# Score and output products of attention issued one by one between the products of the next weight block

## The chip, the cores and the metric

The kernel runs on one core of one Trainium2 chip. The metric is the device time of one execution, in microseconds (us). A core has TensorE (PE in the profile, with its load of stationary operands shown apart as PEld), VectorE (DVE), ScalarE (ACT), GpSimd (POOL) and SyncE (SP), which in this kernel only issues DMAs. Each engine works through its own instructions in the order in which they were written; semaphores make one engine wait for another.

## The reference

A decoder trunk of two layers on 256 positions of width 2048, all in float32. Layer 0 mixes by trailing-window pooling, layer 1 by causal block attention (MoBA) with one block of 256 keys, so that it is plain causal attention over 12 heads of width 128 here. Both layers also have a memory branch: 4 heads that attend to 256 memory tokens. In short:

```python
def memory_attention(mq, mem, w_mem_kv):
    mk, mv = jnp.split(mem @ w_mem_kv, 2, axis=-1)
    ...
    s = jnp.einsum('bshd,bmhd->bhsm', q, k).astype(jnp.float32) * (HEAD_DIM ** -0.5)
    p = jax.nn.softmax(s, axis=-1).astype(v.dtype)
    return jnp.einsum('bhsm,bmhd->bshd', p, v).reshape(B, S, MEM_WIDTH)
```

Each layer has one input projection into [main branch | its SiLU gate | memory query | its SiLU gate], the two gated branches are put side by side, one output projection follows, then `x = LN(alpha * x + y)`. MoBA's keys and values come from one shared projection of the stream behind layer 0; its scores are masked causally and go through the same softmax and value product.

## The kernel before

Every product is done in three: an operand is split into a high part (ScalarE copies it into the rounded type, line 102) and a low part (VectorE subtracts, line 103), and high x high, high x low and low x high are accumulated. So `mm` at line 98 carries every product.

The work is a list of items, one for each weight block of 1024 columns by 128 rows. `run` walks through the list; step i does this: split the block of item i + 3 (`prep_piece`), issue the loads that are planned for this step, then let item i consume its block, then call the functions that were put down for this step with `later(n, fn)`, n steps ahead. For a projection, consuming is 12 products of 512 columns (two row tiles, two k tiles, three products each, lines 240 to 242) into two accumulators; after the eighth block `done` takes the accumulators over. Split weight blocks have four buffers, so VectorE and ScalarE run at most three blocks ahead of TensorE. A few items carry no products: they only bring in blocks of the last output projection ("keep").

Queries, keys and gates have to be turned: VectorE transposes 32 x 32 blocks, SP writes the tile to DRAM with four DMAs (`via<-tr`, line 260), reads it back one step later (`dd<-via`, line 263), and five steps after `done` it is split (`put`). Values are split straight from the accumulators (`to_values`, tile `vv`) by ScalarE and VectorE when the last value block is done.

Attention works on pairs of heads, `MemPair` for the memory branch and `MobaPair` for layer 1. `plan(pr, a, c)` puts their stages on the steps, counted from the last query block: `a` the 12 score products (tile `s`) with the mask and the maxima on VectorE, `a + 1` the exponentials on ScalarE, `a + 2` the division, `a + 3` the turn of the probabilities through DRAM (`p<-via`), `a + 8` their split into halves (`ph`, `pl`), `c` the 12 output products (tile `o`) and the gating, which writes the input of the output projection (`zf`, `zh`, `zl`). There are two memory layers with two pairs each and three MoBA groups with two pairs each: 10 pairs, so 20 blocks of 12 products. In a memory pair all products have 256 columns; in a MoBA pair half have 256 and half 128, since half of a causal score row is known to be masked. A block of 12 is issued in one piece between the products of step a (or c) and those of the next step. The first pair starts at step 6 and the second at 15; the outputs come at 16 and 25 in memory layers and at 17 and 25 in MoBA groups.

After the last query block come eight blocks of the gate and, in a MoBA group, eight of the values, so the last value block is item 16 of that count; in the second and third group a keep item lies among them, and it is item 17.

PSUM holds four accumulators, one bank for `o`, two for `s` (tile name `s2`) and one for `pt`.

## Time and profile before

| | |
|---|---|
| median of 3 runs | 813.2 us |
| lowest and highest | 812.97 and 815.07 us |
| time of the profiled execution | 814.67 us |
| its span, first to last instruction | 812.9 us |
| TensorE busy in the span | 791.9 us, 3671 products |
| VectorE, ScalarE busy | 546.6 us, 390.3 us |
| granted TensorE clock, mean | 0.995 |

The span of the profiled execution is 1.8 us shorter than its time, and its time is 1.5 us above the median. In a timeline row stand start, length, engine, line, operation, tile written and tiles read, shape and count; a bracket gives the idle time of the engine in front of it and what ended it. The length of a product is its way through the array and longer than the distance from one product to the next, so costs are read from starts.

### The profile page before, as it was taken

How to read it: one execution, taken by the hardware profiler on the slowest of the kernel's cores; microseconds unless marked ns; L12 is line 12 of the kernel's file. 1: busy time of each engine (PE TensorE's matmuls, PEld its weight loads, DVE VectorE, ACT ScalarE, POOL GpSimd, SP SyncE). 2: the span in 40 equal slices, each digit the busy share in tenths (PEclk: the TensorE clock that was granted, in tenths of full speed). 3: DMA queues.
4: the chain of work that ended last, by engine and by line, in shares of the span. 5: the costliest groups of instructions: out<-in, count | busy, mean ns of one | idle time of the engine just before them, and what ended most of it. 6: DMA issues, size and time to landing. Idle time of an engine off the chain costs nothing.

```text
span 812.9 us, 10023 instructions
## 1 busy us (share of the span) xinstructions
PE 791.9 (97%) x3671; PEld 660.1 (81%) x3671; DVE 546.6 (67%) x710; ACT 390.3 (48%) x502; POOL 0.2 (0%) x4
## 2 busy tenths in 40 slices
PE   7999999999999999998999999999999999999996
PEld 6878888888888888886778888888887888878885
DVE  6666676768775665755768867666576656765936
ACT  6545545544454434584545544545454445544510
POOL 0000000000000000000000000000000000000000
PEclk9999999999999999999999999999999999999998
DMA  8999666766687755689998786868574685756632
GB/s 321 365 338 310 204 211 194 253 201 215 211 272 262 250 199 187 211 295 293 385 318 258 257 298 207 284 208 271 182 229 139 199 272 197 245 159 219 207 104 103
DMA packets 96180, 193.69 MB, mean 238 GB/s; under 512 B 8671, under 2 KB 31487, under 8 KB 95871
## 3 DMA queue, kind: packets, MB, share of 16 engines
q1 hardware_dynamic: 94800, 190.61, 70.5%
q10 hardware_dynamic: 1332, 2.46, 0.9%
q8 instruction: 28, 0.46, 0.2%
q14 instruction: 20, 0.16, 0.1%
HBM read 173.37 MB, written 19.66 MB: 237 GB/s over the span
## 4 chain that ended last, share of the span: by engine, by line
PE 85%; DMA 8%; DVE 3%; ACT 2%; SPq 1%; issue 1%; DVEq 0%; ACTq 0%
PE acc L98 80%; DMA via<-tr 3%; PE o L98 2%; PE s L98 2%; DMA dd<-via 2%; DMA p<-via 1%; DMA zh<-in_w_in 1%; DVE wl L103 1%; DMA zl<-in_w_mv 1%; ACT wh L102 1%; SPq L260 1%; ACT p L327 1%; PE pt L98 1%; DVE tr L251 0%; DMA raw<-in_w_mk 0%
## 5 line engine op out<-in xcount | busy, mean ns | idle before, releaser
L98 PE MATMUL acc<-wh,xh 128*128 128x512 f32 x704 | 275.3, 391 | 2.3 <-ACT wh L102 2.3
L98 PE MATMUL acc<-wl,xh 128*128 128x512 f32 x704 | 274.9, 391 | 1.5 <-DVE wl L103 1.5
L98 PE MATMUL acc<-wh,xl 128*128 128x512 f32 x704 | 274.5, 390 | 0.0
L103 DVE TENSOR_TENSOR wl<-raw,wh 128x1024 fp32r<-128x1024 f32 (+4 forms) x155 | 180.7, 1176 | 101.5 <-ACT wh L102 99.7
L102 ACT ACTIVATE wh<-raw 128x1024 fp32r<-128x1024 f32 (+4 forms) x155 | 157.2, 1022 | 160.5 <-PE acc L98 133.7
L98 PEld LDWEIGHTS acc<-wh,xh 128*128 128x128 f32 x704 | 132.6, 188 | 30.3 <-ACT wh L102 3.2
L98 PEld LDWEIGHTS acc<-wl,xh 128*128 128x128 f32 x704 | 132.6, 188 | 29.1 <-DVE wl L103 2.5
L98 PEld LDWEIGHTS acc<-wh,xl 128*128 128x128 f32 x704 | 132.4, 188 | 27.7
L98 PE MATMUL acc<-wl,zh 128*128 128x512 f32 x224 | 87.3, 390 | 0.0
L98 PE MATMUL acc<-wh,zh 128*128 128x512 f32 x224 | 87.3, 390 | 0.0
L98 PE MATMUL acc<-wh,zl 128*128 128x512 f32 x224 | 87.2, 389 | 0.0
L103 DVE TENSOR_TENSOR wl<-zh,wh 128x1024 fp32r<-128x1024 f32 x38 | 46.3, 1222 | 26.4 <-ACT wh L102 26.4
L103 DVE TENSOR_TENSOR wl<-zl,wh 128x1024 fp32r<-128x1024 f32 x39 | 47.4, 1221 | 20.1 <-ACT wh L102 20.0
L98 PE MATMUL acc<-wh,mh 128*128 128x512 f32 (+1 forms) x130 | 51.3, 395 | 5.1 <-ACT wh L102 5.1
L102 ACT ACTIVATE wh<-zl 128x1024 fp32r<-128x1024 f32 x39 | 40.7, 1057 | 28.1 <-PE acc L98 27.6
L102 ACT ACTIVATE wh<-zh 128x1024 fp32r<-128x1024 f32 x38 | 39.8, 1054 | 29.6 <-PE acc L98 28.1
L98 PE MATMUL acc<-wl,mh 128*128 128x512 f32 (+1 forms) x130 | 51.4, 395 | 0.8 <-DVE wl L103 0.8
L98 PE MATMUL acc<-wh,ml 128*128 128x512 f32 (+1 forms) x130 | 50.9, 392 | 0.0
L98 PEld LDWEIGHTS acc<-wl,zh 128*128 128x128 f32 x224 | 42.1, 188 | 8.8 <-DVE wl L103 0.3
L98 PEld LDWEIGHTS acc<-wh,zl 128*128 128x128 f32 x224 | 42.0, 188 | 8.8
L98 PEld LDWEIGHTS acc<-wh,zh 128*128 128x128 f32 x224 | 42.1, 188 | 8.6
L102 ACT ACTIVATE zh<-zf 128x256 fp32r<-128x256 f32 x32 | 12.9, 414 | 49.0 <-DVE zf L338 44.7
(152 smaller groups left out, 731.8 us busy)
## 6 DMA issues: line engine op xcount, KB each, us to landing
raw<-in_w_in SPq DMA_DIRECT2D x59, 512.0 KB, 6.1
raw<-in_w_out SPq DMA_DIRECT2D x58, 512.0 KB, 4.4
via<-tr SPq DMA_DIRECT2D x116, 128.0 KB, 3.1
zh<-in_w_in SPq DMA_DIRECT2D x26, 512.0 KB, 6.9
zl<-in_w_in SPq DMA_DIRECT2D x25, 512.0 KB, 6.6
dd<-via SPq DMA_DIRECT2D x21, 512.0 KB, 4.8
raw<-in_w_mk SPq DMA_DIRECT2D x10, 512.0 KB, 4.9
mh<-in_w_sk SPq DMA_DIRECT2D x10, 512.0 KB, 9.1
```

The source lines that it names most:

```text
L98: nc.tensor.matmul(o, l, r, start=start, stop=stop)
L102: nc.scalar.activation(hi, src, AF.Copy)
L103: nc.vector.tensor_sub(lo, src, f(hi))
L260: nc.sync.dma_start(st["via"][:, :, i].rearrange("j r x -> r j x"), tr[32 * i:32 * i + 32, :, :n])
L327: nc.scalar.activation(dst, src, AF.Exp, bias=self.nb[:, c:c + 1], scale=SCALE, accum_out=self.sm[:, c:c + 1])
```

## The change

Score and output products are no longer issued by their stage. The stage puts them into a queue, `woven`, and the next projection item takes one out behind each of its own 12 products of 512 columns. What used to follow the products within the stage becomes a stage of its own one step later, which first empties the queue: `scored` (mask, maxima) behind the scores and `gate` (gating, split) behind the outputs. Exponentials, division, turn and halves move one step with it. The outputs' step c changes for some pairs: from 17 to 18 for the first pair of each MoBA group, from 25 to 26 for the second pair everywhere, while the first pair of the memory layers stays at 16. Arithmetic, number and shapes of the products and the DMAs stay the same.

```diff
+    woven = deque()
+
+    def weave_mm(*args):
+        woven.append(args)
+
+    def tick():
+        if woven:
+            mm(*woven.popleft())
+
+    def flush():
+        while woven:
+            tick()
...
-                            mm(acc[t][:, s], xh, h[:, kk, s], first, False)
-                            mm(acc[t][:, s], xh, l[:, kk, s], False, False)
-                            mm(acc[t][:, s], xl, h[:, kk, s], False, last)
+                            for st, wt, a0, a1 in ((xh, h, first, False), (xh, l, False, False), (xl, h, False, last)):
+                                mm(acc[t][:, s], st, wt[:, kk, s], a0, a1)
+                                tick()
...
+        def gate(self):
+            flush()
+            for j in range(2):
+                gated(self.o[:, j], self.st["g"][:, self.h0 + j, :], self.kt0 + j)
...
         def a(self):
             q, k = self.st["q"], self.st["k"]
-            s = ps.tile([P, 2, 2, T], F32, name="s2")
+            s = self.s = ps.tile([P, 2, 2, T], F32, name="s2")
...
-                    mm(s[:, j, t], qh, k[:, 0, h], True, False)
-                    mm(s[:, j, t], qh, k[:, 1, h], False, False)
-                    mm(s[:, j, t], ql, k[:, 0, h], False, True)
+                    weave_mm(s[:, j, t], qh, k[:, 0, h], True, False)
+                    weave_mm(s[:, j, t], qh, k[:, 1, h], False, False)
+                    weave_mm(s[:, j, t], ql, k[:, 0, h], False, True)
+
+        def scored(self):
+            flush()
+            s = self.s
...
-                    mm(o[:, j], vh, self.ph[:, e], m == 0, False)
-                    mm(o[:, j], vh, self.pl[:, e], False, False)
-                    mm(o[:, j], vl, self.ph[:, e], False, m == 1)
-            for j in range(2):
-                gated(o[:, j], g[:, self.h0 + j, :], 12 + self.h0 + j)
+                    weave_mm(o[:, j], vh, self.ph[:, e], m == 0, False)
+                    weave_mm(o[:, j], vh, self.pl[:, e], False, False)
+                    weave_mm(o[:, j], vl, self.ph[:, e], False, m == 1)
...
     def plan(pr, a, c):
 
-        later(a, pr.a)
-        later(a + 1, pr.exps)
-        later(a + 2, pr.divide)
-        later(a + 3, pr.b)
-        later(a + 8, pr.halves)
+        for n, fn in enumerate((pr.a, pr.scored, pr.exps, pr.divide, pr.b)):
+            later(a + n, fn)
+        later(a + 9, pr.halves)
         later(c, pr.c)
+        later(c + 1, pr.gate)
...
             plan(prs[0], 6, 16)
-            plan(prs[1], 15, 25)
+            plan(prs[1], 15, 26)
...
-            plan(prs[0], 6, 17)
-            plan(prs[1], 15, 25)
+            plan(prs[0], 6, 18)
+            plan(prs[1], 15, 26)
```

`MobaPair` is changed in the same way as `MemPair`.

## The prediction

> **What bounds the kernel now.** I read the page first, then the waits of TensorE, then the timeline of TensorE around each of the places that the change touches. The page and the waits give:

> ```profile
> PE 791.9 (97%) x3671; PEld 660.1 (81%) x3671; DVE 546.6 (67%) x710; ACT 390.3 (48%) x502; POOL 0.2 (0%) x4
> ...
> PE acc L98 <- ACT wh L102: 7.4, 3, 5.1
> PE o L98 <- DVE vv L103: 1.8, 2, 0.9
> PE s L98 <- DVE qq L103: 0.8, 1, 0.8
> PE o L98 <- ACT vv L102: 0.6, 2, 0.4
> ```

> TensorE is busy for 97% of the span, so only two things can move the time: what a product costs in the stream, and the few microseconds in which TensorE stands still. Of the waits, three belong to score products `s` and output products `o`, 1.8 + 0.8 + 0.6 = 3.2 us. The waiting list counts only idle time; the cost of a stop is read from the distances between starts, which also hold the slow restart. A row of the timeline is the start, the length, the operation, and in brackets the idle time before it. The worst stop is that of the outputs in the second MoBA group:

> ```profile
> 614.48 0.39 PE L98 MATMUL acc<-wh,xl 128*128 128x512 f32 x1
> 615.10 0.39 PE L98 MATMUL o<-ph,vv 128*128 128x256 f32 x1 [0.23 <-ACT vv L102]
> 615.33 0.28 PE L98 MATMUL o<-pl,vv 128*128 128x256 f32 x1
> 616.49 0.44 PE L98 MATMUL o<-ph,vv 128*128 128x256 f32 x2 [0.88 <-DVE vv L103]
> 616.77 0.27 PE L98 MATMUL o<-pl,vv 128*128 128x128 f32 x1
> 617.09 0.49 PE L98 MATMUL o<-ph,vv 128*128 128x128 f32 x2
> ...
> 617.00:622.00 5.00, 4.96 (x19) 4.15 (x19) 2.57 (x10) 1.78 (x3) 0.00 (x0) 0.66 0.00 0
> ...
> 700.00:715.00 15.00, 13.70 (x71) 11.23 (x70) 10.56 (x16) 7.26 (x16) 0.00 (x0) 1.00 0.52 192
> ```

> The outputs follow the last product of the values directly, so they wait until ScalarE and VectorE have split those values. The last two rows are sums over stretches of time, and the number after the engines' busy times is the granted clock. From 617 to 622, right behind the stop, it is 0.66 on average; around the like stop at 711 it is 1.00.

> **The unit costs.** In the fences of this part stand an output block of a memory pair, a score block and the rest of an output block of MoBA pairs, none of them with a wait:

> ```profile
> 145.34 0.39 PE L98 MATMUL acc<-wh,xh 128*128 128x512 f32 x1
> ...
> 146.02 0.28 PE L98 MATMUL o<-ph,vv 128*128 128x256 f32 x1
> 146.13 0.28 PE L98 MATMUL o<-pl,vv 128*128 128x256 f32 x1
> ...
> 147.45 0.40 PE L98 MATMUL acc<-wh,xh 128*128 128x512 f32 x1
> 147.68 0.40 PE L98 MATMUL acc<-wl,xh 128*128 128x512 f32 x1
> ...
> 148.84 0.39 PE L98 MATMUL acc<-wh,xh 128*128 128x512 f32 x1
> ```

> ```profile
> 584.72 1.54 PE L98 MATMUL s<-kk,qq 128*128 128x128 f32 x12
> 586.10 0.40 PE L98 MATMUL acc<-wh,xh 128*128 128x512 f32 x1
> ...
> 641.64 0.34 PE L98 MATMUL o<-ph,vv 128*128 128x256 f32 x2
> 641.82 0.28 PE L98 MATMUL o<-pl,vv 128*128 128x128 f32 x1
> ...
> 642.74 0.44 PE L98 MATMUL acc<-wh,xh 128*128 128x512 f32 x1
> 643.02 0.40 PE L98 MATMUL acc<-wl,xh 128*128 128x512 f32 x1
> ```

> A 512-column product takes (146.02 - 145.34)/3 = 0.227 us. A 256-column one takes (147.45 - 146.02)/12 = 0.119. In the MoBA block six have 256 columns and six 128: (586.10 - 584.72)/12 = 0.115 on average, so a 128-column product takes 0.11 there, hardly less than twice the columns do. Something other than columns, about 0.11 us a product, holds it: the load of the next stationary block.

> **The change, part by part.**

> 1. *Alternation.* Twenty blocks of 12 products (8 of memory pairs, 12 of MoBA pairs) give 96 + 72 = 168 products of 256 columns and 72 of 128. No trace of before has long and short products in turn, so I bound it by the edges of blocks. Going in, the first 256-column product lasts 146.13 - 146.02 = 0.11; coming out, the first 512-column product lasts 147.68 - 147.45 = 0.23. A pair is 0.34, against 0.227 + 0.119 = 0.346 now. For 128 columns: behind a longer product it lasts (641.82 - 641.64) - 0.12 = 0.06, but the 512-column product behind a 128-column one lasts 643.02 - 642.74 = 0.28, since the load that the short product did not cover is paid there. Pair 0.34, now 0.227 + 0.11 to 0.115. So alternation is worth nothing in the likely case: the long product hides the short one's load, and the next long one's load stands behind the short product. Lower bound: every 256-column product at 0.113, 168 x 0.006 = 1.0 us won. Upper bound: the six products from 147.45 to 148.84 take 1.39 against 1.36, 0.03 us a block; half of that for every alternating pair is 240 x 0.015 = 3.6 lost, but since the two ends of a pair read 0.34, I cut this at 1.9 and take +0.1.

>  [...]

> 2. *Outputs of the second and third MoBA group.* They are queued one step later and then issued behind products of the step after it. Today's loss at 614: from the values' last product to the first output 615.10 - 614.48 - 0.227 = 0.39; 615.10 to 615.33 is 0.10 too long; 615.33 to 616.49 is 1.04 too long; 616.49 to 616.77 covers two products, 0.10 too long; 616.77 to 617.09 is 0.20 too long. Sum 1.83. The third group is the same:

> ```profile
> 710.64 0.39 PE L98 MATMUL acc<-wh,xl 128*128 128x512 f32 x1
> 711.40 0.39 PE L98 MATMUL o<-ph,vv 128*128 128x256 f32 x1 [0.37 <-ACT vv L102]
> 711.63 0.28 PE L98 MATMUL o<-pl,vv 128*128 128x256 f32 x1
> 712.79 0.45 PE L98 MATMUL o<-ph,vv 128*128 128x256 f32 x2 [0.88 <-DVE vv L103]
> 713.08 0.27 PE L98 MATMUL o<-pl,vv 128*128 128x128 f32 x1
> 713.39 0.49 PE L98 MATMUL o<-ph,vv 128*128 128x128 f32 x2
> ...
> 609.45 0.96 DVE L409 TENSOR_TENSOR p<-s,mask 128x768 f32<-128x768 f32 x1 [0.64 <-PE s L98]
> 610.44 1.01 DVE L322 TENSOR_REDUCE small<-p 128x2 f32<-128x256 f32 x2
> ...
> 615.75 1.28 DVE L103 TENSOR_TENSOR vv<-acc,vv 128x512 fp32r<-128x512 f32 x2
> ```

>  0.53 + 0.10 + 1.04 + 0.11 + 0.20 = 1.98. What covers it: after the values' last product at 614.48 comes a whole weight block (12 x 0.227 = 2.72 us) and one product more, so the first output starts at about 617.66; the split of the values ends at 617.03. The mask and maxima of the second pair, now one step later, stand on VectorE ahead of it: 12 products of scores and 12 of weights end about 612, plus 0.96 + 1.01 + 0.17 gives 614.4, a weight split (1.23, as long as the split of the same size at 419.85 below) to 615.6, values to 616.9. The low part is asked for by the third output only, at 618.35. Covered, by 1.4 us. If that cover were gone, the 1.83 and 1.98 would come back.

> 3. *The half clock.* 5 x (1 - 0.66) = 1.70 us of the profiled execution went into it. It began within a microsecond of the stop; that the stop at 711 had none behind it shows that a stop does not always bring it. Without a stop I expect none there; 0 and 1.70 are the bounds, and I take the 1.70.

>  [...]

> 4. *Scores of the second memory layer.*

> ```profile
> 419.36 0.39 PE L98 MATMUL acc<-wh,xl 128*128 128x512 f32 x1
> 419.87 0.50 PE L98 MATMUL s<-kk,qq 128*128 128x256 f32 x2
> 421.13 1.45 PE L98 MATMUL s<-kk,qq 128*128 128x256 f32 x10 [0.76 <-DVE qq L103]
> ...
> 419.85 1.23 DVE L103 TENSOR_TENSOR qq<-dd,qq 128x1024 fp32r<-128x1024 f32 x1 [3.18 <-ACT qq L102]
> ```

>  Loss now: 419.87 - 419.36 - 0.227 = 0.28, and 421.13 - 419.87 - 2 x 0.12 = 1.02, together 1.30. The queries come from a DMA, so their low half still ends at 419.85 + 1.23 = 421.08. The third score product is the first to read it; alternating, it would start at 419.59 + 3 x 0.227 + 2 x 0.12 = 420.5. It waits about 0.57, and with 0.10 for the slow restart, as in part 2, 0.67 stays: 0.63 won. Bounds: 0 to 1.30.

> 5. *Everything a step later.* Score reduction, exponentials, division, turn and halves all move one step, with their DMAs on SP's queue, and keep their distances from one another; no weight load passes another. VectorE stands in the same place relative to TensorE as now, waiting for scores (0.64 idle at 609.45), so its cover of later weight blocks is unchanged. One distance shrinks. In memory layers the first pair's outputs stay at step 16 while its halves move from 14 to 15, and the second pair's `scored` empties the queue in step 16, so these two blocks are not alternated at all. In the second memory layer the halves end, with the wait for their DMA, about 3.4 us ahead of the outputs:

> ```profile
> 446.51 1.23 DVE L103 TENSOR_TENSOR pl<-p,ph 128x1024 fp32r<-128x1024 f32 x1 [1.02 <-ACT ph L102]
> ...
> 451.11 0.28 PE L98 MATMUL o<-ph,vv 128*128 128x256 f32 x1
> ```

>  451.11 - 447.74 = 3.4, less one step of 2.72 leaves 0.7. Cost 0 if that holds, up to 1 us if the DMA is late; I take 0.25. The gate of the last group, a step or two later, lies at least three weight blocks ahead of the products that read it: nothing.

> Sum against the profiled execution's own 814.67 (its span is 812.9, and the 1.8 around it stay): -1.83 - 1.98 - 1.70 - 0.63 + 0.1 + 0.25 = -5.8, so 808.9. The median of the three runs is 813.2, 1.5 below the profiled one, nearly the half-clock loss; if those runs had none, 813.2 - 4.44 + 0.35 = 809.1. Both readings meet at 809.0.

> **The rivals.**

> - *The half clock appears elsewhere, or stays* (808.9 + 1.7 = 810.6). For it: the stops of TensorE for weights (7.4 us in the list) are untouched and could be hit. Against: they were not hit in this execution. 15%.
> - *Loads run two ahead.* Then a 128-column product costs 0.06 and nothing is paid behind it: 72 x 0.055 = 4.0, so 805.0. For it: the 0.06 above. Against: the 0.28 that follows. 7%. [...]
> - *The waits move.* VectorE gets to the values only after the mask and maxima; if it is over 1.4 us later than worked out, half of 1.83 + 1.98 comes back with part of the scores' wait, and with late halves in the second memory layer: 811.3 to 813. 14%.
> - *Slower: each change of length exposes a load.* If the 0.28 behind a 128-column product (0.057 above 0.227) is paid behind every short product, with no gain going in, it costs 240 x 0.057 = 13.7: 822.6. It turns the forecast into a loss from 4.2/240 = 0.018 us a pair. For it: that row, and the 0.03 after each block. Against: behind 256 columns the row shows 0.23. 14%.

> **How the numbers follow.** Forecast 809.0 with 50%. I call no change what lies within 0.3% (2.4 us, about what a measurement of this kernel can tell), 810.8 to 815.6. Faster: 50 + 7 + two thirds of 15 = 67%; no change: 5 + 14 and 1 of the slower rival = 20%; slower 13%. The range: downwards all of the 256-column gain (1.0), the whole score wait (0.67), none of the 0.35, and the lowest of the three runs as the base (0.2), 806.8; upwards the half clock and most of the moved waits, 812.2. Left out are two-ahead loads and the slower rival, 21%.

> **What would show it.** Waits of `o` on `vv` gone and that of `s` on `qq` down to about 0.6 us; no granted clock under 1.00 at 617; in an alternating block 12 pairs in 4.1 us (256 columns) and 4.1 (MoBA): much less speaks for loads two ahead, over 4.4 for the slower rival. A new wait of `o` on `pl` near 450, or of weights on ScalarE behind a block, would prove me wrong in part 5.

## The result, and the profile after

| | before | after |
|---|---|---|
| median, 13 runs each, in turn | 815.07 us | 811.25 us |
| lowest to highest | 812.97 to 819.53 | 809.68 to 813.82 |
| ratio of the times, 95% interval | | 0.9949 (0.9931 to 0.9967) |
| profiled execution, its span | 814.67, 812.9 | 812.46, 810.7 |
| granted TensorE clock, mean | 0.995 | 0.992 |

The change makes the kernel faster by 0.5%. The forecast was 809.0 against 813.2, a ratio of 0.9948. The median of before rose to 815.07 when more runs of it were made, so the absolute time lies 2 us above the forecast and the difference, 3.8 us, beside the 4.2 forecast.

The list of waits of TensorE in the kernel after, whole (engine, tile, line, what ended the wait, us in total, times, the longest):

```profile
PE acc L98 <- ACT wh L102: 6.2, 2, 5.0
PE acc L98 <- DVE wl L103: 3.9, 5, 2.4
PE pt L908 <- DVE cc L905: 2.7, 1, 2.7
PE acc L98 <- ACT cct L910: 0.4, 1, 0.4
```

No score product and no output product waits any more. Two of the four rows are waits for weights, and the other two (`pt` and `cct`, at 804 us) belong to the last normalization at the end of the kernel; three rows of `s` and `o` with 3.2 us are gone. To read what that was worth I take, in each kernel, the same two 512-column products on either side of a place and the time from one to the other. Between the two stands the same work in both kernels, so the difference is what the place costs. The timeline of TensorE before, two products around the scores of the second memory layer, then around the outputs of the second and the third MoBA group:

```profile
418.23 0.39 PE L98 MATMUL acc<-wh,xh 128*128 128x512 f32 x1
...
426.53 0.39 PE L98 MATMUL acc<-wh,xh 128*128 128x512 f32 x1
...
613.35 0.39 PE L98 MATMUL acc<-wh,xh 128*128 128x512 f32 x1
...
626.45 0.39 PE L98 MATMUL acc<-wh,xh 128*128 128x512 f32 x1
...
709.51 0.39 PE L98 MATMUL acc<-wh,xh 128*128 128x512 f32 x1
...
721.11 0.39 PE L98 MATMUL acc<-wh,zh 128*128 128x512 f32 x1
```

The same products in the timeline after:

```profile
421.26 0.39 PE L98 MATMUL acc<-wh,xh 128*128 128x512 f32 x1
...
428.18 0.39 PE L98 MATMUL acc<-wh,xh 128*128 128x512 f32 x1
...
615.54 0.39 PE L98 MATMUL acc<-wh,xh 128*128 128x512 f32 x1
...
625.17 0.39 PE L98 MATMUL acc<-wh,xh 128*128 128x512 f32 x1
...
708.45 0.39 PE L98 MATMUL acc<-wh,xh 128*128 128x512 f32 x1
...
718.08 0.39 PE L98 MATMUL acc<-wh,zh 128*128 128x512 f32 x1
```

The scores' stretch went from 8.30 to 6.92 us, the outputs of the second group from 13.10 to 9.63, those of the third from 11.60 to 9.63 (9.636 without rounding): 1.38 + 3.47 + 1.97 = 6.8 us won. But blocks that never waited became longer. Where TensorE alternates, the timeline after shows, first in a memory pair and then in a MoBA pair:

```profile
116.18 0.28 PE L98 MATMUL s<-kk,qq 128*128 128x256 f32 x1
116.29 0.40 PE L98 MATMUL acc<-wl,xh 128*128 128x512 f32 x1
...
120.06 0.28 PE L98 MATMUL s<-kk,qq 128*128 128x256 f32 x1
...
587.02 0.22 PE L98 MATMUL s<-kk,qq 128*128 128x128 f32 x1
587.08 0.45 PE L98 MATMUL acc<-wl,xh 128*128 128x512 f32 x1
587.36 0.22 PE L98 MATMUL s<-kk,qq 128*128 128x128 f32 x1
...
587.70 0.22 PE L98 MATMUL s<-kk,qq 128*128 128x128 f32 x1
```

Eleven pairs of 256 and 512 columns take 120.06 - 116.18 = 3.88 us, 0.353 a pair, where the two kinds in blocks of their own take 0.119 + 0.227 = 0.346. A pair of 128 and 512 takes 0.34: the short product lasts 587.08 - 587.02 = 0.06 and the long one behind it 587.36 - 587.08 = 0.28. By the same kind of stretch, a memory block or a block of MoBA scores that alternates costs 0.060 us more (memory scores 6.900 to 6.960, memory outputs 9.620 to 9.680, MoBA scores 6.833 to 6.893) and a block of MoBA outputs 0.083 (9.553 to 9.636). Of the 20 blocks 18 alternate, since the first pair's outputs in the memory layers are flushed in one piece: 12 x 0.060 + 6 x 0.083 = 1.2 us. Of that, 0.99 lies outside the three stretches above, so the places that the change touches come to -6.8 + 1.0 = -5.8 us.

The two profiled executions differ by only 814.67 - 812.46 = 2.2 us. Most of the missing 3.6 is in the stretch between the two layers (from the first product of the second layer's memory values to the first of its eighth query block), which the change leaves alone: 46.91 us before (355.00 to 401.91), 49.77 after (355.17 to 404.94). One wait is longer there in this execution, and after it two stretches of 3.41 us run at half clock (374.20 to 377.62 and 391.27 to 394.69). The timeline after, and sums over stretches of time (start, end, length; busy time and instructions of TensorE, its loads, VectorE, ScalarE, GpSimd; mean granted clock; DMA share; GB/s):

```profile
372.89 0.50 PE L98 MATMUL acc<-wl,mh 128*128 128x512 f32 x1 [2.38 <-DVE wl L103]
```

```profile
374.00:378.00 4.00, 4.00 (x12) 3.17 (x11) 1.22 (x1) 2.94 (x5) 0.00 (x0) 0.57 1.00 306
391.00:395.00 4.00, 3.81 (x10) 3.02 (x11) 4.00 (x5) 2.67 (x3) 0.00 (x0) 0.57 1.05 408
...
614.00:622.00 8.00, 8.00 (x40) 6.70 (x40) 6.01 (x11) 5.91 (x13) 0.00 (x0) 1.00 0.44 166
```

The clock behind the second group's outputs is now 1.00 where it was 0.66. Between the layers 4.00 x 0.43 + 4.00 x 0.43 = 3.4 us are lost to the clock. In another execution of the same kernel (after_again, below) that stretch took 46.62 without a halved window, so this is a matter of the single execution and not of the change. It isn't rare: of the eleven traces of this case five have a halved window there (after, outputs_18, threes, woven_early, long_stop_filled), and before has none.

### The profile page after: what moved, and what is told of

It reads as the page before. It is cut to its first block, busy times and chain, and to the rows that moved or that the text cites. A ratio compares the mean times of both kernels' runs of the same rounds, so it can differ in the third digit from the quotient of the medians.

```text
span 810.7 us, 10039 instructions
## 1 busy us (share of the span) xinstructions
PE 793.0 (98%) x3671; PEld 661.0 (82%) x3671; DVE 546.7 (67%) x710; ACT 389.9 (48%) x502; POOL 0.2 (0%) x4
## 4 chain that ended last, share of the span: by engine, by line
PE 89%; DMA 6%; DVE 2%; SPq 1%; ACT 1%; issue 1%; ACTq 0%; DVEq 0%
PE acc L98 84%; DMA via<-tr 3%; PE o L98 2%; PE s L98 2%; DVE wl L103 1%; DMA raw<-in_w_mk 1%; DMA dd<-via 1%; DMA raw<-in_w_out 1%; ACT wh L102 1%; PE pt L98 1%; DMA p<-via 0%; SPq L273 0%; SPq L150 0%; DVE xl L103 0%; SPq L148 0%
## 5 line engine op out<-in xcount | busy, mean ns | idle before, releaser
L98 PE MATMUL acc<-wl,xh 128*128 128x512 f32 x704 | 276.4, 393 | 1.0 <-DVE wl L103 1.0
L98 PE MATMUL acc<-wh,xh 128*128 128x512 f32 x704 | 276.1, 392 | 1.2 <-ACT wh L102 1.2
L98 PE MATMUL acc<-wh,xl 128*128 128x512 f32 x704 | 276.4, 393 | 0.0
L103 DVE TENSOR_TENSOR wl<-raw,wh 128x1024 fp32r<-128x1024 f32 (+4 forms) x155 | 180.6, 1176 | 96.4 <-ACT wh L102 94.5
L102 ACT ACTIVATE wh<-raw 128x1024 fp32r<-128x1024 f32 (+4 forms) x155 | 157.1, 1022 | 150.4 <-PE acc L98 116.4
L98 PEld LDWEIGHTS acc<-wh,xh 128*128 128x128 f32 x704 | 132.6, 188 | 29.6 <-ACT wh L102 1.7
L98 PEld LDWEIGHTS acc<-wl,xh 128*128 128x128 f32 x704 | 132.5, 188 | 29.3 <-DVE wl L103 2.1
L98 PEld LDWEIGHTS acc<-wh,xl 128*128 128x128 f32 x704 | 132.6, 188 | 27.9
L98 PE MATMUL acc<-wl,zh 128*128 128x512 f32 x224 | 87.5, 391 | 0.3 <-DVE wl L103 0.3
L98 PE MATMUL acc<-wh,zl 128*128 128x512 f32 x224 | 87.5, 390 | 0.0
L98 PE MATMUL acc<-wh,zh 128*128 128x512 f32 x224 | 87.4, 390 | 0.0
L103 DVE TENSOR_TENSOR wl<-zh,wh 128x1024 fp32r<-128x1024 f32 x38 | 46.4, 1224 | 32.4 <-ACT wh L102 30.8
L103 DVE TENSOR_TENSOR wl<-zl,wh 128x1024 fp32r<-128x1024 f32 x39 | 47.1, 1219 | 20.4 <-ACT wh L102 20.4
L102 ACT ACTIVATE wh<-zh 128x1024 fp32r<-128x1024 f32 x38 | 40.0, 1057 | 38.3 <-PE acc L98 36.2
L98 PE MATMUL acc<-wh,mh 128*128 128x512 f32 (+1 forms) x130 | 51.8, 398 | 5.0 <-ACT wh L102 5.0
L102 ACT ACTIVATE wh<-zl 128x1024 fp32r<-128x1024 f32 x39 | 40.7, 1055 | 32.2 <-PE acc L98 32.1
L98 PE MATMUL acc<-wl,mh 128*128 128x512 f32 (+1 forms) x130 | 52.1, 401 | 2.6 <-DVE wl L103 2.6
L98 PE MATMUL acc<-wh,ml 128*128 128x512 f32 (+1 forms) x130 | 51.3, 395 | 0.0
L98 PEld LDWEIGHTS acc<-wl,zh 128*128 128x128 f32 x224 | 42.1, 188 | 9.4 <-DVE wl L103 0.7
L98 PEld LDWEIGHTS acc<-wh,zl 128*128 128x128 f32 x224 | 42.0, 188 | 8.8
L98 PEld LDWEIGHTS acc<-wh,zh 128*128 128x128 f32 x224 | 42.1, 188 | 8.7
L102 ACT ACTIVATE zh<-zf 128x256 fp32r<-128x256 f32 x32 | 13.0, 415 | 53.2 <-DVE zf L329 48.7
```

Source lines behind the costliest of these rows:

```text
L98: nc.tensor.matmul(o, l, r, start=start, stop=stop)
L102: nc.scalar.activation(hi, src, AF.Copy)
L103: nc.vector.tensor_sub(lo, src, f(hi))
```

## The experiments

My theory was: the gain is the step, that is, the outputs come late enough for the split, and the queries' scores too; alternating short with long products gains nothing and costs a little. The rival: alternation itself hides loads or waits, and the step only makes room for it. A third question was what brings the half clock.

### The step without the alternation (late_block, late_block_2), and the kernel after once more (after_again)

```diff
                                 mm(acc[t][:, s], st, wt[:, kk, s], a0, a1)
-                                tick()
```

Everything stays where the kernel after has it, but each block of 12 is issued in one piece by the stage that empties the queue. The second run was made beside the kernel after on another chip.

> Every stage stands on the same step as in the changed kernel, but nothing is issued behind the 512-column products: each block of 12 goes out in one piece where the queue is emptied. Theory (the later step ends the waits, alternation costs a little): waits of o on vv and of s on qq stay away, and against the changed kernel each alternating block gets 0.06 to 0.08 us shorter, 1.2 us in all, so about 3.0 to 5 us under the kernel before. Rival (alternation is what pays): the blocks get no shorter and the waits or the block costs come back, 1 to 4 us slower than the changed kernel.

> Steps of the changed kernel, blocks in one piece, again beside the changed kernel. Theory (alternation costs 1.2 us): 1 to 2.5 us under the changed kernel's median. Rival (the difference of the first look was chance): within 0.5 us of it.

> The changed kernel once more, so that the next two stand beside it on one chip. [...]

Measured: 808.74 us against 815.74, ratio 0.9914 (0.9891 to 0.9938). On the second chip 809.39 against 816.44, 0.9923 (0.9900 to 0.9945), with the kernel after at 810.45, 0.9929 (0.9908 to 0.9951). Beside the kernel after that is 810.45 - 809.39 = 1.06 us less, but the intervals overlap, so the times alone don't separate the two; the stretches do. The outputs of the second group in the timeline of late_block:

```profile
613.56 0.39 PE L98 MATMUL acc<-wh,xh 128*128 128x512 f32 x1
...
623.12 0.39 PE L98 MATMUL acc<-wh,xh 128*128 128x512 f32 x1
```

They take 9.56 us, against 13.10 before and 9.63 after. All undisturbed stretches are back at the lengths of before (6.900, 9.620, 6.833, 9.554), no `s` and no `o` waits, and the scores of the second memory layer take 6.90. So in these stretches the step alone does it all, and the alternation is a loss of 1.2 us. In after_again the scores' stretch was 7.65 instead of 6.92, with this row in its list of waits:

```profile
PE s L98 <- DVE qq L103: 0.3, 1, 0.3
```

Alternating products begin a block early, and then the scores still meet the split of queries that came by DMA; how late these are differs from one execution to the next. A block issued a step later didn't wait in either execution.

### One number alone (outputs_18)

```diff
 # in the kernel before
-            plan(prs[0], 6, 17)
+            plan(prs[0], 6, 18)
```

The kernel before with the first MoBA pair's outputs one step later, and nothing else.

> The kernel before with one number changed: the outputs of the first pair of each MoBA group at step 18 in place of 17, still in one block. Theory: the waits of o on vv (1.83 and 1.98 us with their restarts) go, so 3.8 us under the kernel before where no clock is halved; the wait of s on qq (about 1.4) stays; no alternation cost. Rival (the gain needs the queue): under 1 us.

Measured: 810.62 against 815.74, 0.9937 (0.9913 to 0.9961), as much as the whole change. From its timeline, the scores of the second memory layer and the outputs of the second group:

```profile
417.73 0.39 PE L98 MATMUL acc<-wh,xh 128*128 128x512 f32 x1
...
419.92 1.45 PE L98 MATMUL s<-kk,qq 128*128 128x256 f32 x10 [0.43 <-DVE qq L103]
...
425.32 0.39 PE L98 MATMUL acc<-wh,xh 128*128 128x512 f32 x1
...
612.13 0.39 PE L98 MATMUL acc<-wh,xh 128*128 128x512 f32 x1
...
621.69 0.39 PE L98 MATMUL acc<-wh,xh 128*128 128x512 f32 x1
```

The outputs take 9.56 us: one step is cover enough. The scores still wait, but here the stretch is 7.59, a loss of 0.69 against the 1.40 of before. So the loss at the scores is 0.7 or 1.4 in one and the same order of work, by when the queries land.

### The alternation without the step (woven_early)

```diff
-            plan(prs[1], 15, 26)
+            plan(prs[1], 15, 25)
...
-            plan(prs[0], 6, 18)
-            plan(prs[1], 15, 26)
+            plan(prs[0], 6, 17)
+            plan(prs[1], 15, 25)
```

> The changed kernel with the steps of the outputs as before (17 and 25 in MoBA groups, 25 for the second memory pair), so alternation is kept and the extra step is taken back. Theory: in the second and third MoBA group the first output stands one 512-column product behind the values' last, at 0.23 us, and the third output needs the low part some 1.4 to 1.9 us behind it: about 1 us of waiting with its restart comes back in each, 2 us in all over the changed kernel. Rival (alternation itself hides the split of the values): no wait on vv, time as the changed kernel.

Measured: 812.74 over 12 runs against 815.74, 0.9964 (0.9948 to 0.9980). A row of its list of waits, and one of its timeline:

```profile
PE o L98 <- DVE vv L103: 0.8, 2, 0.4
```

```profile
616.48 0.38 PE L98 MATMUL o<-ph,vv 128*128 128x256 f32 x1 [0.38 <-DVE vv L103]
```

The third output, the first that reads the low half, waits again, once in each of the two groups. Their stretches take 10.28 and 10.29, 0.65 over the 9.64 of after. So with the old steps the alternation makes up two thirds of the stop by itself (the 1.85 to 2.05 of before become 0.65), since three long products now stand ahead of the first output that reads a low half; the step takes the rest. I had expected some 2 us to come back, and 1.3 did.

### Three at a time (threes)

```diff
                                 mm(acc[t][:, s], st, wt[:, kk, s], a0, a1)
-                                tick()
+                            for _ in range(3):
+                                tick()
```

If each change of length costs, four changes a block instead of twelve must cost a third.

> The changed kernel, but three short products are issued behind every three long ones, so a third as many changes of length. If each change of length costs, the 1.2 us that alternation costs in the trace falls to about 0.4, and a block of 12 long and 12 short products gets 0.04 to 0.05 us shorter than with single ones. If a short product costs by itself wherever it stands, the blocks stay as long. Waits as in the changed kernel.

Measured: 810.15 against 815.74, 0.9931 (0.9907 to 0.9954). The timeline of threes around the scores of a memory pair and of a MoBA pair:

```profile
88.88 0.39 PE L98 MATMUL acc<-wh,xh 128*128 128x512 f32 x1
...
95.80 0.39 PE L98 MATMUL acc<-wh,xh 128*128 128x512 f32 x1
...
584.10 0.39 PE L98 MATMUL acc<-wh,xh 128*128 128x512 f32 x1
...
591.00 0.39 PE L98 MATMUL acc<-wh,xh 128*128 128x512 f32 x1
```

Inside the MoBA block, three products of 128 columns in a row and the long one behind them:

```profile
586.14 0.44 PE L98 MATMUL s<-kk,qq 128*128 128x128 f32 x3
586.43 0.44 PE L98 MATMUL acc<-wh,xh 128*128 128x512 f32 x1
586.71 0.40 PE L98 MATMUL acc<-wl,xh 128*128 128x512 f32 x1
```

The memory block takes 6.92, so 0.02 over the 6.90 of one piece instead of 0.06: a third, as expected. The MoBA scores stay at 6.90, 0.06 over 6.83, and the MoBA outputs lose 0.05 to 0.06. So the count of changes explains the pairs of 256 columns and not those with 128: the three short products take 586.43 - 586.14 = 0.29 and not 3 x 0.06, and the long one behind them still 0.28, so a row of three costs as much as three single ones. A load that is paid behind every short product fits this, but no run changes the loads alone. In all about 0.8 us is left instead of the 0.4 that I had expected.

### Filling the wait between the layers (late_fill)

```diff
 # in late_block
+                if j == fill:
+                    pt = ps.tile([P, 512], F32, name="pt")
+                    for _ in range(5):
+                        mm(pt, sta.kt(2 * kb)[0][:, :P], h[:, 0], True, True)
...
-        proj(memT, [a["w_mv"][layer, kb] for kb in range(8)], to_values(v))
+        proj(memT, [a["w_mv"][layer, kb] for kb in range(8)], to_values(v), fill=7 if layer else None)
...
-        proj(xT, w_in(layer, 6), to_heads(q))
+        proj(xT, w_in(layer, 6), to_heads(q), fill=2 if layer else None)
```

late_block, with five more 512-column products, whose result nobody reads, behind the last value block and five behind the third query block of the second memory layer, where TensorE stands still for weights.

> Blocks in one piece as before this one, and 10 products more that compute nothing that is used: five of 512 columns into a spare PSUM bank behind the last value block of the second memory layer and five behind the third query block, in front of the two places where TensorE stands still longest between the layers (1.2 to 2.4 us). [...]

Measured: 808.56 against 816.44, 0.9910 (0.9885 to 0.9936); of its six runs one, at 882.9 with a granted clock of 0.85, lies far from the other five (807.8 to 809.9, median 808.26), for a reason that no trace shows; the ratio leaves it out. The stretch of 35 us between the layers, in late_fill and then in late_block_2:

```profile
365.00:400.00 35.00, 32.86 (x142) 26.22 (x141) 21.36 (x22) 19.17 (x25) 0.00 (x0) 1.00 0.97 334
```

```profile
365.00:400.00 35.00, 29.95 (x128) 23.34 (x127) 20.42 (x20) 19.05 (x25) 0.00 (x0) 1.00 0.94 331
```

No half clock with the filling, but none without it either in this execution, so the run can't say whether filling prevents it. It costs nothing that can be measured: these ten products stand where TensorE waited anyway. late_block and late_fill are the fastest versions measured, and their intervals don't tell them apart.

### A stop made longer (long_stop), and filled (long_stop_filled)

```diff
 # in the kernel before
+            for _ in range(again):
+                nc.vector.tensor_sub(dst()[:, t, 1], acc, f(dst()[:, t, 0]))
...
-        proj(xT, [a["w_sv"][grp, kb] for kb in range(8)], to_values(v))
+        proj(xT, [a["w_sv"][grp, kb] for kb in range(8)], to_values(v, 3))
```

VectorE writes the low half of each MoBA value tile four times instead of once, so that the outputs wait longer. In the filled version 16 products of 512 columns whose result is not read stand in front of the first pair's outputs:

```diff
+            if self.h0 == 0:
+                q, k = self.st["q"], self.st["k"]
+                pt = ps.tile([P, 512], F32, name="pt").rearrange("p (a b) -> p a b", a=2)
+                for _ in range(16):
+                    mm(pt, q[:, 0, 0, :P], k[:, 0, 0:2], True, True)
```

> The kernel before, in which VectorE writes the low part of each MoBA value tile four times instead of once (same numbers), so that the stop of TensorE in front of the first pair's outputs gets about 3.6 us longer in each of the three groups, some 10 us in all. Theory (a free-running window of 3.41 us in which products of fewer than about six times 512 columns run brings half the clock in the next): the stops leave such a window in nearly every phase, so two or three half-clock windows right behind them, 1.7 us each, on top of the 10 us. Rival (the half clock seen at 617 had nothing to do with the stop): none behind them, only the 10 us.

> The same, with 16 products of 512 columns whose result is not used (3.6 us) issued in front of those outputs, inside the stop. The outputs come no earlier, but TensorE works through most of the wait. Theory: no half-clock window behind the three places, so 3 to 5 us under the unfilled kernel. Rival (it is the wait itself, or chance): half-clock windows as often as without, equal time.

Measured: long_stop 834.08 against 814.3, 1.0241 (1.0211 to 1.0272); filled 828.36, 1.0161 (1.0125 to 1.0197). A wait and two stretches behind the stops of long_stop:

```profile
PE o L98 <- DVE vv L308: 12.9, 6, 3.1
```

```profile
622.00:629.00 7.00, 5.13 (x16) 4.36 (x17) 4.09 (x11) 1.78 (x3) 0.00 (x0) 0.51 0.00 0
...
721.00:731.30 10.30, 7.10 (x21) 5.95 (x22) 7.26 (x16) 1.78 (x3) 0.00 (x0) 0.50 0.00 0
```

Waits of 12.9 us come with two halved windows in a row behind the second group and three behind the third: 7.00 x 0.49 + 10.30 x 0.50 = 8.6 us of lost clock, though in part while TensorE stood still. Behind the first group's stop there was none. The filled version:

```profile
PE o L98 <- DVE vv L308: 4.4, 2, 2.2
```

```profile
616.00:622.00 6.00, 6.00 (x28) 4.99 (x27) 4.08 (x6) 3.53 (x11) 0.00 (x0) 1.00 0.43 143
...
623.46:626.87 3.41, 1.44 (x10) 1.35 (x11) 2.23 (x4) 0.00 (x0) 0.00 (x0) 1.00 0.00 0
626.87:630.29 3.42, 3.42 (x10) 2.65 (x9) 2.42 (x10) 1.78 (x3) 0.00 (x0) 0.50 0.00 0
```

The first part of the stop is filled and has the full clock behind it. A second part, 2.2 us before the second pair of values is there, I had overlooked; it brought one halved window behind the stop of the second group and one behind that of the third, against the "none" that I had expected. By the medians the version with 16 needless products in each group is 834.08 - 828.36 = 5.7 us faster than the one without, and the granted clock of every execution goes the same way: 0.979 to 0.987 without the filling, 0.990 to 0.995 with it. The two traced executions don't show the gain: they took 829.69 and 829.31, and the first is the fastest of its five, with the highest clock among them. So that filling saves part of the half clock is shown by the clocks on record, and where the 5.7 us lie is not shown by a trace.

## Why the prediction was right, point by point

The forecast held: faster, by 4.2 us forecast and 3.8 measured, and 811.25 lies within the range of 806.8 to 812.2. The sum for the places touched, -5.8, is what the stretches of the two profiled executions give, -5.8. But it came out so by luck, because three errors of terms cancelled: the scores gave 0.75 more and the 0.25 was not needed, and the alternation took 1.1 more. The absolute time is also less sure than it looks. The base of 813.2 was the median of three runs, and on that base 811.25 lies in the band from 810.8 to 815.6 that the prediction calls no change; only against the 815.07 of more runs is the gain clear.

1. *Alternation, +0.1: mis-sized; measured +1.2.* The figures for 128 columns were exact (0.06, then 0.28, a pair of 0.34). For 256 columns I took a pair from the two edges of a block, 0.11 and 0.23, and so rounded 0.353 to 0.34. That is what failed: a difference of 0.007 us a pair, counted over 168 products, can't be read from starts with two decimals; it needs a row over many pairs, and before has none. My block edge of 0.03 was nearer: half of it a pair gave the upper bound, which I cut to 1.9 and which held.
2. *Outputs of the groups, -1.83 and -1.98: right.* Without the alternation (late_block) the two stretches shrink by 3.55, that is 1.85 beside the half clock of 1.70, and by 2.05. The cover was there, 1.64 us against the 1.4 worked out (in after the split of the values ends at 618.91 and the third output starts at 620.55), no `o` waits on `vv`, and outputs_18 shows that this one step is enough.
3. *Half clock, -1.70: right at its place, not in the sum.* The clock from 614 to 622 is 1.00 in this trace, as in after_again and late_block. But in the profiled execution two halved windows appeared between the layers: my first rival (15%, 810.6) is what this execution did, by a stop for weights as the rival said, with two windows in place of the one that it priced; five of the eleven traces have such a window there, which speaks for a chance above 15%. After the start-up the longest idle time of TensorE before the first halved window was 2.38 us in this trace.
4. *Scores of the second memory layer, -0.63: one of two cases.* Measured 1.38 won in the profiled execution and 0.65 in after_again (8.30 to 7.65). The landing of the queries' DMA decides; I had taken one landing time as fixed. Counted from the start of the last query product, the split that waits for this DMA begins after 13.6 us in after (407.43 to 420.99) and in outputs_18, and after 14.0 to 14.5 us in the other nine traces (14.4 in before). So 0.63 was right for the usual landing, and the 1.38 is the luck of one execution.
5. *A step later, +0.25: not needed.* No wait of `o` on `pl` is in the list after. The 0.7 us that I had left for it were enough.

Without the half clock the terms as measured give -1.85 - 2.05 - (0.65 to 1.40) + 1.2, so -3.4 to -4.1. That is as much as the whole difference of the medians, 3.8. But on the second chip the difference was 816.44 - 810.45 = 6.0 us, and there the granted clock of every execution is on record: 0.9933 on average over the eleven of before, 0.9963 over the six of after. The difference of 0.0030, times 814 us, is 2.4 us, an estimate of what more half clock cost before, wherever it fell, and rather too high, since part of it can fall where TensorE stands still. With it the terms come to 5.8 to 6.5. For the first measurement it stays open what the half clock cost before: the clocks of its runs of before are not on record, but for the profiled one (the thirteen of after average 0.9947), and the interval of the ratio, -2.7 to -5.6 us, leaves room for none of the 1.70 and for all of it.

Of the other rivals, loads two ahead is refuted by the 0.28 that the long product behind each 128-column one takes. The slower rival, a load exposed by each change of length, had the direction of the loss right and is in keeping with threes for 256 columns, though the loads themselves were never varied; it was wrong by its size: it turns the forecast round from 0.018 us a pair, and measured are 1.2/(18 x 12) = 0.0056. The moved waits came back only where the step was undone, in woven_early.

## What to carry to other kernels

Where a product waits for an operand that another engine has still to split, put its whole block a step later before thinking of anything finer: one changed number gave here what the whole change gave (810.62 us, a ratio of 0.9937 against 0.9949). Issuing short products singly between long ones hid part of a stop where the step was too early (1.85 to 2.05 us became 0.65), but where nothing waited it only cost, 0.06 to 0.08 us a block, and without it the kernel is at 808.7 to 809.4 us. When an edit removes a wait of a microsecond, look at the clock behind the wait as well: behind the second group's outputs it was 0.66 in before (617 to 622 us) and 1.00 in after (614 to 622).

## What the runs showed of the hardware that I had not expected

```profile
614.19:617.60 3.41, 2.25 (x13) 1.45 (x12) 2.42 (x3) 1.34 (x3) 0.00 (x0) 1.00 0.36 130
617.60:621.02 3.42, 3.42 (x12) 2.84 (x12) 1.59 (x5) 1.27 (x3) 0.00 (x0) 0.50 0.00 0
...
709.76:713.17 3.41, 2.15 (x11) 1.41 (x9) 2.26 (x3) 2.07 (x5) 0.00 (x0) 1.00 0.00 0
713.17:716.58 3.41, 3.37 (x21) 2.83 (x19) 1.35 (x4) 0.79 (x3) 0.00 (x0) 1.00 0.00 0
```

The first, with 2,991 columns, is followed by 0.50; the second, with 3,528, by 1.00, though TensorE is busy for less of it (2.15 against 2.25 us): in these two, busy time doesn't tell which is followed by the half clock, and the columns do. The window that was followed by it had 3.41 - 2.25 = 1.16 us of idle time. My estimate from these counts is that where a stop falls among the windows decides; in before the second group's stop was hit and the third's was not. This is in keeping with the wider spread of before (812.97 to 819.53) against that of late_block and late_block_2 (808.21 to 809.7, 808.62 to 811.9), whose traces have no halved window between the start-up and 790 us. After's execution shows the same between the layers:

```profile
387.86:391.27 3.41, 1.41 (x6) 0.64 (x4) 1.36 (x2) 3.41 (x6) 0.00 (x0) 1.00 0.93 327
391.27:394.68 3.41, 3.41 (x8) 2.70 (x9) 3.41 (x4) 2.40 (x3) 0.00 (x0) 0.50 1.05 408
```

Six products in the first window, 2,216 columns, and half the clock in the next. These counts are of two executions and of products of one type. They show what stood ahead of a half clock here; what sets the clock is not shown, and the loads, which go with the products, are not told apart from them.
